# Delta-rule layer of a four-layer decoder trunk: the substitution's transfers move from SyncE's queue to GpSimd's, one per diagonal block, and two of its tiles are used a second time

## The chip, the cores and the metric

The kernel runs on one core of a Trainium2 chip. The metric is device time in microseconds for one execution of the whole program. The time before is 860.16 us, the median of three runs (860.01 to 860.22).

## The reference

Four pre-norm residual layers act on 256 tokens of width 1024, in float32, and a final RMSNorm follows. The layers are a pooling mixer, a gated delta-rule mixer, latent attention, and a pooling mixer again. Only the second layer matters here. For 8 heads, in chunks of 64 tokens, its core is

```python
decay = jnp.exp(jnp.where(causal, diff, -jnp.inf))
L = jnp.where(strict, jnp.einsum('bhnid,bhnjd->bhnij', k_beta, k) * decay, 0.0)
A = jnp.eye(C, dtype=L.dtype) + L
rhs = jnp.concatenate([v_beta, k_beta * jnp.exp(g)[..., None]], axis=-1)
sol = lax.linalg.triangular_solve(A, rhs, left_side=True, lower=True)
```

A scan over the chunks with a 128 x 256 state per head follows. So a unit lower triangular matrix has to be inverted, or a system solved with it, for each head and chunk.

## The kernel before, in words

The 256 tokens are two tiles of 128 (`NT = 2`, index `t`). All weight matrices are streamed from HBM in units of 128 x 512 slices through three raw buffers. ScalarE rounds each slice to a high part (`whi`, line 117), VectorE or, for a few slices, GpSimd makes the low part (`wlo`, line 119), and TensorE does three matmuls per product (lines 127 to 129, and 167). The ring of `whi` and `wlo` has nine slices each. The weight loads are issued by SyncE (SP, line 104).

The delta-rule layer is `gdn_layer`. It works with chunks of 128 tokens, one per tile `t`, so there are 2 x 8 = 16 triangular matrices of 128 x 128. Their transposes lie in `LT` (line 696), written on VectorE at line 692, heads 0 to 3 and then 4 to 7, for both `t`. The inverse is made in two steps.

`substitution` (line 712) inverts the 32 x 32 diagonal blocks, four per matrix, 64 in all. The blocks lie spread over 128 partitions; they are brought together with one block per partition. Eight transfers (line 718, one per `t` and diagonal position `d`) write the blocks of `LT` to the HBM buffer `d_l`, and one transfer (line 721) reads them into `Lb`, 64 partitions x 4 KB. Then GpSimd does forward substitution in 31 rounds of two instructions: a product `pr` (line 726) and a subtraction from `Tb` (line 730). One transfer (line 732) writes `Tb` to the HBM buffer `d_t`, and eight transfers (line 736) bring the inverted blocks back to the diagonals of the two tiles `T[0]` and `T[1]`. All these transfers are issued by SP, in whose queue the weight loads also stand; each queue is issued in order.

`inverses` (line 787) joins the blocks. VectorE transposes `T` to `U` (line 797), and `pairs(t)` (line 803) makes 64 x 64 blocks: TensorE multiplies `LT` by `T` (line 806), VectorE masks the result into `X1` (line 808), TensorE multiplies again (line 812), and VectorE subtracts (line 815). `whole(t)` (line 817) does the same to 128 x 128, at lines 820 to 833. `news` then applies `U[0]` to the values (line 847). `X1` (line 794) is a pair of tiles of their own; a third of each is set to zero by GpSimd (line 796).

The program text lists the steps of the layer in one order:

```python
order = "g0 k0 d a0 g1 k1 a1 s q0 v0 i v1 v2 q1 g2 u0 v3 u1 g3".split()
```

Here `g` are gate projections, `k`, `q`, `v` the projections of keys, queries and values, `a` the making of `LT`, `s` the substitution, `i` the inverses and `u` the use of them. This is only the order in which the instructions are written down. The library's scheduler (`schedule_with_timeline_sim=True`, line 1242) fixes the order of each engine's instructions and of each queue's transfers before the run, by its own prices for every instruction. It also chooses how many buffers a tag gets and where each tile lies (`auto_bufs=True`). On the chip each engine works through its fixed order and waits on semaphores. Tiles made by `big` share the tag `s4` (line 70), whose count is left to the scheduler.

Of the kernel before, what the change touches and what calls it, by code (L numbers as in the profile page):

```python
# [16 lines left out]
P = 128  # L17
D = 1024
S = 256
NT = S // P  # L20
# [22 lines left out]
def trunk(ctx: ExitStack, tc: tile.TileContext, x, positions, norm_g, pool_w_in, pool_w_grp,  # L43
          pool_scale, pool_w_out, gdn_w_in, gdn_conv, gdn_a_log, gdn_dt_bias, gdn_norm_g,
          gdn_w_out, mla_w_in, mla_q_norm_g, mla_w_uq, mla_kv_norm_g, mla_w_ukv, mla_w_out,
          final_g, out, depth=4, final=True):
    nc = tc.nc
# [22 lines left out]
    def big(name, *dims, dt=F32):  # L70
        return s4.tile([P, *dims], dt, tag="s4", name=name)
# [463 lines left out]
    def gdn_layer(i, j, hT):  # L535
        H = GDN_H
        M = NT * H
# [72 lines left out]
        for t in range(NT):  # L610
            nc.gpsimd.dma_start(
                out=Gb[t].rearrange("p h s -> p (h s)"),
# [28 lines left out]
        Q, B = 4, 32  # L641
        Tb = big("Tb", B, B)[:M * Q]
        nc.gpsimd.memset(Tb, 0.0)
        nc.gpsimd.memset(Tb.rearrange("m r c -> m (r c)")[:, ::B + 1], 1.0)
        T = [big("T", H, P) for _ in range(NT)]
        for t in range(NT):
# [48 lines left out]

        LT = [big("LT", H, P) for _ in range(NT)]

# [10 lines left out]
        def lower(hf):  # L708
            for t in range(NT):
                against(LT, kT, s2, hf, t)  # L710

        def substitution():

            d_l = dram.tile([M * Q, B * B], F32, name="d_l")
            lv = d_l.rearrange("(t m d) (r c) -> t d r m c", t=NT, d=Q, r=B)
            for t in range(NT):
                for d in range(Q):
                    nc.sync.dma_start(out=lv[t, d],
                                      in_=LT[t][d * B:(d + 1) * B, :, d * B:(d + 1) * B])
            Lb = big("Lb", B, B)[:M * Q]  # L720
            nc.sync.dma_start(out=Lb, in_=d_l.rearrange("m (r c) -> m r c", r=B))
            pr = small("pr", 256, bufs=1)[:M * Q]
# [8 lines left out]
            d_t = dram.tile([M * Q, B * B], F32, name="d_t")  # L731
            nc.sync.dma_start(out=d_t.rearrange("m (r c) -> m r c", r=B), in_=Tb)
            tv = d_t.rearrange("(t m d) (r c) -> t d r m c", t=NT, d=Q, r=B)
            for t in range(NT):
                for d in range(Q):
                    nc.sync.dma_start(out=T[t][d * B:(d + 1) * B, :, d * B:(d + 1) * B],
                                      in_=tv[t, d])
            nc.vector.reciprocal(rki, rk)
# [48 lines left out]
        def inverses():  # L787
# [5 lines left out]
            U.extend(big("U", H, P) for _ in range(NT))  # L793
            X1 = [big("X1", H, P) for _ in range(NT)]
            for t in range(NT):
# [457 lines left out]
```

## Time and profile before

| | |
|---|---|
| median of three runs | 860.16 us |
| the profiled execution | 859.14 us |
| its span, first to last instruction | 857.4 us |
| mean granted TensorE clock | 0.990 |
| transfers on SP's queue (q1) | 109056 packets, 138.17 MB |
| transfers on GpSimd's queue (q0) | 320 packets, 1.06 MB |
| substitution, first `pr` to last `Tb` | 259.78 to 310.09 us |

The profile is one execution. PE is TensorE's matmuls, PEld its weight loads, DVE is VectorE, ACT ScalarE, POOL GpSimd, SP SyncE; POOLq and SPq are transfer issues on these engines' queues. A group or a timeline row gives the line of the kernel, the operation, what is written from what is read, and the shape; in brackets stand the idle time just before it and what ended it. Tile names in the rows are the program's names with numbers left out, so `X1` is shown as `X`. A row `lhs <- rhs: a, n, b` in the table of waits says that the left waited for the right, a us in total, n times, b us at the longest. A "landing" is the time from a transfer's issue to the arrival of its data. The granted clock is the share of full TensorE speed that the chip allowed.

### The profile page before, as it was taken

Reading aid. Unit: us, or ns where it says so; the run is one execution under the profiler, and the core shown is the slowest. Engines: PE = TensorE matmul, PEld = TensorE weight load, DVE = VectorE, ACT = ScalarE, POOL = GpSimd, SP = SyncE. Lnnn points to the kernel's source line nnn. Section 1 sums busy time; section 2 is a strip of 40 time slices with the busy share of each in tenths; the row PEclk is TensorE's granted clock in tenths of the full one; section 3 lists DMA queues with packets and bytes.
Section 4 is the critical chain, followed back from the end, with each engine's and each line's share of the span. In section 5 each row is a group of like instructions: output and inputs, shape, how many; then the busy total and the mean of one; then the engine's idle time right before and its main releaser. Section 6 shows DMA issues by size and latency. Waiting matters only on the chain.

```text
span 857.4 us, 16137 instructions
## 1 busy us (share of the span) xinstructions
PE 835.0 (97%) x5967; PEld 778.7 (91%) x5967; DVE 591.2 (69%) x1138; ACT 488.2 (57%) x1007; POOL 155.7 (18%) x292
## 2 busy tenths in 40 slices
PE   7999999999999969999999999999999999999996
PEld 6999998988999959888979998999989989999986
DVE  4589776456989665656577659778767668866852
ACT  5565555467857435555565654566555476555542
POOL 4000000233248941022212002000000210000012
PEclk9999999999999989999999999999999999999999
DMA  6765556546555462222547676743652547565551
GB/s 199 249 188 188 178 189 213 180 148 206 188 160 176 134 168 102 75 74 99 173 147 215 201 165 172 196 132 95 171 167 79 173 149 218 175 192 183 187 200 50
DMA packets 111288, 140.43 MB, mean 164 GB/s; under 512 B 23340, under 2 KB 53224, under 8 KB 111208
## 3 DMA queue, kind: packets, MB, share of 16 engines
q1 hardware_dynamic: 109056, 138.17, 53.1%
q8 instruction: 47, 0.77, 0.4%
q0 software_dynamic: 320, 1.06, 0.3%
q10 hardware_dynamic: 1832, 0.16, 0.2%
q14 instruction: 33, 0.27, 0.1%
HBM read 137.79 MB, written 1.58 MB: 163 GB/s over the span
## 4 chain that ended last, share of the span: by engine, by line
PE 85%; POOL 7%; DVE 2%; DMA 2%; issue 2%; ACT 1%; SPq 1%; POOLq 0%; ACTq 0%; DVEq 0%
PE acc L167 34%; PE acc L127 12%; PE acc L128 12%; PE acc L129 12%; POOL Tb L730 2%; POOL pr L726 2%; PE aux L127 2%; PE aux L128 2%; PE aux L129 2%; DVE h L303 1%; DMA gain<-in_norm_g_dram 1%; PE aux L688 1%; ACT junk L209 1%; PE aux L806 1%; PE tp L1165 1%
## 5 line engine op out<-in xcount | busy, mean ns | idle before, releaser
L119 DVE TENSOR_TENSOR wlo<-raw,whi 128x512 fp32r<-128x512 f32 (+1 forms) x491 | 338.6, 712 | 163.2 <-ACT whi L117 160.9
L117 ACT CAST whi<-raw 128x512 fp32r<-128x512 f32 (+1 forms) x508 | 301.4, 617 | 261.8 <-PE acc L167 89.8
L127 PE MATMUL acc<-hTh,whi 128*128 128x256 f32 x832 | 235.3, 283 | 1.0 <-DVE cv L636 1.0
L128 PE MATMUL acc<-hTl,whi 128*128 128x256 f32 x832 | 235.8, 283 | 0.0
L129 PE MATMUL acc<-hTh,wlo 128*128 128x256 f32 x832 | 234.7, 282 | 0.0
L127 PEld LDWEIGHTS acc<-hTh,whi 128*128 128x128 f32 x832 | 157.7, 190 | 1.8 <-issue 1.4
L128 PEld LDWEIGHTS acc<-hTl,whi 128*128 128x128 f32 x832 | 157.6, 189 | 0.4
L129 PEld LDWEIGHTS acc<-hTh,wlo 128*128 128x128 f32 x832 | 157.5, 189 | 0.2
L167 PE MATMUL acc<-wlo,yTh 128*128 128x256 f32 (+1 forms) x384 | 116.2, 319 | 0.0
L167 PE MATMUL acc<-whi,yTh 128*128 128x256 f32 (+1 forms) x384 | 116.2, 323 | 0.0
L167 PE MATMUL acc<-whi,yTl 128*128 128x256 f32 (+1 forms) x384 | 92.4, 321 | 0.0
L167 PEld LDWEIGHTS acc<-wlo,yTh 128*128 128x128 f32 x384 | 72.0, 188 | 5.0
L167 PEld LDWEIGHTS acc<-whi,yTh 128*128 128x128 f32 x384 | 71.9, 188 | 5.2
L167 PEld LDWEIGHTS acc<-whi,yTl 128*128 128x128 f32 x384 | 63.1, 188 | 5.6
L291 POOL TENSOR_TENSOR hg<-x,gain 128x256 f32<-128x256 f32 x18 | 14.8, 832 | 259.1 <-DVE x L353 257.4
L167 PE MATMUL acc<-wlo,hTh 128*128 128x512 f32 (+1 forms) x144 | 55.9, 394 | 0.4 <-DVE wlo L119 0.2
L167 PE MATMUL acc<-whi,hTh 128*128 128x512 f32 (+1 forms) x144 | 55.5, 393 | 0.7 <-ACT hTh L195 0.7
L167 PE MATMUL acc<-whi,hTl 128*128 128x512 f32 (+1 forms) x144 | 45.4, 388 | 0.0
L119 POOL TENSOR_TENSOR wlo<-raw,whi 128x512 fp32r<-128x512 f32 x17 | 23.1, 1360 | 70.2 <-ACT whi L117 70.2
L434 POOL COPY win<-u 128x4 f32<-128x4 f32 x8 | 2.8, 354 | 177.0 <-ACT u L428 177.0
L167 PEld LDWEIGHTS acc<-wlo,hTh 128*128 128x128 f32 x144 | 27.3, 190 | 6.8 <-DVE wlo L119 1.7
L167 PEld LDWEIGHTS acc<-whi,hTh 128*128 128x128 f32 x144 | 27.3, 190 | 6.8 <-ACT hTh L195 1.7
(337 smaller groups left out, 1443.3 us busy)
## 6 DMA issues: line engine op xcount, KB each, us to landing
raw<-in_pool_w_in_dram SPq DMA_DIRECT2D x60, 512.0 KB, 4.4
raw<-in_gdn_w_in_dram SPq DMA_DIRECT2D x48, 512.0 KB, 3.9
raw<-in_pool_w_out_dram SPq DMA_DIRECT2D x32, 512.0 KB, 3.7
raw<-in_mla_w_in_dram SPq DMA_DIRECT2D x24, 512.0 KB, 4.4
raw<-in_mla_w_uq_dram SPq DMA_DIRECT2D x36, 256.0 KB, 3.8
raw<-in_pool_w_grp_dram SPq DMA_DIRECT2D x16, 512.0 KB, 4.2
raw<-in_gdn_w_out_dram SPq DMA_DIRECT2D x16, 512.0 KB, 3.5
raw<-in_mla_w_ukv_dram SPq DMA_DIRECT2D x32, 256.0 KB, 3.4
```

Source lines behind the costliest of these rows:

```text
L117: a = nc.scalar.copy(hi, v)
L119: b = e.tensor_tensor(out=lo, in0=v, in1=hi.bitcast(F32), op=ALU.subtract)
L127: nc.tensor.matmul(o, lhsT=lhs[0], rhs=rhs[0], start=start, stop=False)
L128: nc.tensor.matmul(o, lhsT=lhs[0], rhs=rhs[1], start=False, stop=False)
L129: nc.tensor.matmul(o, lhsT=lhs[1], rhs=rhs[0], start=False, stop=stop)
L167: nc.tensor.matmul(o, lhsT=act(k, t * P, P)[x], rhs=parts[j][z][:, sl], start=k == first and x == z == 0, stop=k == last and x == 1)
L209: nc.scalar.activation(junk[:, :n], src, AF.Square, scale=scale, accum_out=o)
L291: nc.gpsimd.tensor_tensor(out=self.early[t, a], in0=xs[t][:, sl], in1=self.g[:, sl], op=ALU.mult)
L303: nc.vector.scalar_tensor_tensor(out=h[:, cut:], in0=xs[t][:, sl], scalar=r[:, 0:1], in1=self.g[:, sl], op0=ALU.mult, op1=ALU.mult)
L688: nc.tensor.matmul(ps[:, b], lhsT=kT[hf][:, b, tt], rhs=rhs[hf][:, b, tt], start=True, stop=True)
L726: nc.gpsimd.tensor_tensor(out=pv, op=ALU.mult, in0=Lb[:, r, r + 1:, None].to_broadcast([M * Q, n, c]), in1=Tb[:, r:r + 1, :c].to_broadcast ...
L730: nc.gpsimd.tensor_tensor(out=tv, in0=tv, in1=pv, op=ALU.subtract)
```

## The change

The two tiles `T` become halves of one tile `Ts`, and the two tiles `LT` halves of one tile `LTs`. One transfer can then carry the block at diagonal position `d` for both `t` and all heads, so the eight transfers each way become four with twice the bytes. All ten are issued by GpSimd. `Lb` and `Tb` are kept as whole 128-partition tiles, and after the substitution their memory is viewed as `X1`, so that no tiles are made for `X1`.

```diff
-        Tb = big("Tb", B, B)[:M * Q]
+        Tb_ = big("Tb", B, B)
+        Tb = Tb_[:M * Q]
...
-        T = [big("T", H, P) for _ in range(NT)]
+        Ts = big("T", NT, H, P)
+        T = [Ts[:, t] for t in range(NT)]
+
+        def diagonal(a, d):
+
+            return a[d * B:(d + 1) * B, :, :, d * B:(d + 1) * B].rearrange("p t h c -> p (t h) c")
...
-        LT = [big("LT", H, P) for _ in range(NT)]
+        LTs = big("LT", NT, H, P)
+        LT = [LTs[:, t] for t in range(NT)]
...
+        free = []
+
         def substitution():
 
             d_l = dram.tile([M * Q, B * B], F32, name="d_l")
-            lv = d_l.rearrange("(t m d) (r c) -> t d r m c", t=NT, d=Q, r=B)
-            for t in range(NT):
-                for d in range(Q):
-                    nc.sync.dma_start(out=lv[t, d],
-                                      in_=LT[t][d * B:(d + 1) * B, :, d * B:(d + 1) * B])
-            Lb = big("Lb", B, B)[:M * Q]
-            nc.sync.dma_start(out=Lb, in_=d_l.rearrange("m (r c) -> m r c", r=B))
+            lv = d_l.rearrange("(m d) (r c) -> d r m c", d=Q, r=B)
+            for d in range(Q):
+                nc.gpsimd.dma_start(out=lv[d], in_=diagonal(LTs, d))
+            Lb_ = big("Lb", B, B)
+            Lb = Lb_[:M * Q]
+            free.extend((Lb_, Tb_))
+            nc.gpsimd.dma_start(out=Lb, in_=d_l.rearrange("m (r c) -> m r c", r=B))
...
-            nc.sync.dma_start(out=d_t.rearrange("m (r c) -> m r c", r=B), in_=Tb)
-            tv = d_t.rearrange("(t m d) (r c) -> t d r m c", t=NT, d=Q, r=B)
-            for t in range(NT):
-                for d in range(Q):
-                    nc.sync.dma_start(out=T[t][d * B:(d + 1) * B, :, d * B:(d + 1) * B],
-                                      in_=tv[t, d])
+            nc.gpsimd.dma_start(out=d_t.rearrange("m (r c) -> m r c", r=B), in_=Tb)
+            tv = d_t.rearrange("(m d) (r c) -> d r m c", d=Q, r=B)
+            for d in range(Q):
+                nc.gpsimd.dma_start(out=diagonal(Ts, d), in_=tv[d])
...
-            X1 = [big("X1", H, P) for _ in range(NT)]
+
+            X1 = [a.rearrange("p (h a) c -> p h (a c)", h=H) for a in free]
```

## The prediction, made before the result was known

> **What bounds the kernel now.** I read the page's busy table first, then the table by stretches, TensorE's waits, and the timelines of the stretch in which TensorE waits.
>
> ```profile
> PE 835.0 (97%) x5967; PEld 778.7 (91%) x5967; DVE 591.2 (69%) x1138; ACT 488.2 (57%) x1007; POOL 155.7 (18%) x292
> ```
> ```profile
> 190.00:308.70 118.70, 117.73 (x901) 112.24 (x899) 96.38 (x213) 76.17 (x144) 69.88 (x88) 1.00 0.58 176
> 308.70:316.10 7.40, 0.04 (x2) 0.04 (x1) 1.90 (x3) 1.91 (x4) 1.41 (x5) 0.85 0.55 134
> 316.10:324.60 8.50, 8.50 (x42) 8.50 (x43) 4.88 (x6) 3.33 (x9) 0.00 (x0) 0.53 0.66 200
> 324.60:361.00 36.40, 36.40 (x271) 32.11 (x270) 22.91 (x47) 18.77 (x42) 4.86 (x6) 1.00 0.27 88
> 435.00:685.00 250.00, 250.00 (x1786) 232.98 (x1784) 178.64 (x387) 143.35 (x333) 15.97 (x26) 1.00 0.57 161
> 694.00:846.00 152.00, 152.00 (x1141) 145.00 (x1140) 103.92 (x157) 82.95 (x143) 8.50 (x17) 1.00 0.57 181
> ```
> ```profile
> PE aux L806 <- DMA T<-d_t: 7.4, 1, 7.4
> ```
>
> TensorE is the bound. Its column is the first after the width of a stretch; the granted clock is the third from the end. From 435 to 685 and from 694 to 846 us it is never idle, so nothing can be gained there. The one large gap lies in the stretch that the change touches: 7.4 us in which TensorE stands at line 806 and waits for the transfers of T. After it the clock is 0.53 for 8.5 us, which loses 8.5 x 0.47 = 4.0 us. The stall and its aftermath together cost 11.4 us, 1.3% of the time, and this is the most that the change can win.
>
> The chain that ends in the stall:
>
> ```profile
> 248.11 2.14 DVE L692 SCALAR_TENSOR_TENSOR LT<-aux,s,DT 128x128 f32<-128x128 f32 x8
> ```
> ```profile
> 249.25 1.82 SPq L718 DMA_DIRECT2D d_l<-LT  x4
> 251.18 0.39 SPq L104 DMA_DIRECT2D raw<-in_gdn_w_in_dram  x1
> 251.61 1.95 SPq L718 DMA_DIRECT2D d_l<-LT  x4
> ...
> 300.12 5.42 SPq L104 DMA_DIRECT2D raw<-in_gdn_w_in_dram  x3
> 310.12 0.47 SPq L732 DMA_DIRECT2D d_t<-Tb  x1
> 310.68 0.53 SPq L104 DMA_DIRECT2D raw<-in_gdn_w_in_dram  x1
> 313.12 3.78 SPq L736 DMA_DIRECT2D T<-d_t  x8
> ```
> ```profile
> 253.11 2.87 DMA d_l<-LT
> 256.10 3.62 DMA Lb<-d_l
> ...
> 310.12 2.94 DMA d_t<-Tb
> 313.98 2.02 DMA T<-d_t
> ```
> ```profile
> 259.78 0.23 POOL L726 TENSOR_TENSOR pr<-Lb,Tb 64x31 f32<-64x31 f32 x1 [1.25 <-DMA Lb<-d_l]
> ...
> 309.85 0.24 POOL L730 TENSOR_TENSOR Tb<-Tb,pr 64x31 f32<-64x31 f32 x1
> ```
> ```profile
> 308.45 0.28 PE L129 MATMUL acc<-hTh,wlo 128*128 128x256 f32 x1
> 316.09 3.65 PE L806 MATMUL aux<-T,LT 128*128 128x64 f32 x16 [7.36 <-DMA T<-d_t]
> ...
> 326.57 1.89 PE L806 MATMUL aux<-T,LT 128*128 128x64 f32 x16
> ```
>
> LT is whole at 250.25. Eight transfers, one collecting transfer and GpSimd's 62 steps follow, from 259.78 to 310.09, then d_t and eight transfers back, and line 806 starts at 316.09. The second group of 16 matmuls of that line takes 1.89 us where the first took 3.65: that is the clock. TensorE's order is fixed before the run, and it had independent projection matmuls left (they fill 316 to 350). So the stall is not the length of the chain. It is the error of the plan, which put line 806 about 7.4 us too early. A longer chain costs nothing if the plan knows of it; a chain that is longer than planned costs its whole excess.
>
> **The change part by part.** First the real length of the chain. The only transfers that GpSimd issues now give the price:
>
> ```profile
> 206.15 0.80 POOL L608 DMA_DIRECT2D d_g<-grow  x1 [0.95 <-DVE grow L606]
> 208.34 1.09 POOL L611 DMA_DIRECT2D Gb<-d_g  x2 [1.39 <-DMA d_g<-grow]
> ```
> ```profile
> Gb<-d_g POOLq DMA_DIRECT2D x2, 512.0 KB, 6.5
> d_l<-LT SPq DMA_DIRECT2D x8, 32.0 KB, 3.0
> ...
> T<-d_t SPq DMA_DIRECT2D x8, 32.0 KB, 2.0
> ...
> d_g<-grow POOLq DMA_DIRECT2D x1, 8.0 KB, 1.9
> ```
>
> An issue on GpSimd takes 0.80 alone and 1.09/2 = 0.55 behind another; on SP it takes 0.45.
>
> Front: a merged transfer reads both halves of LT, so the first starts at 250.25 and not at 249.25: +1.00. The last of four starts 0.80 + 2 x 0.55 = 1.90 later, at 252.15, and not at 253.11 (eight issues with weight loads among them): -0.96 in all. I keep the landing of 2.87, because nothing shows 64 KB from GpSimd; the bounds are 1.9 (d_g) and 6.5 (Gb, eight times the bytes). Lb pays 0.80 for 0.53 at issue: +0.27, with the same bounds. GpSimd's steps start 0.69 us earlier.
>
> Back: d_t pays 0.80 for 0.47: +0.33. Its data come from GpSimd's own last step, so no other queue is woken. Line 806 needed the first four of eight transfers, 316.09 - 313.12 = 2.97 after the first issue. It now needs all four, since each carries both halves: 1.90 to the last issue and 2.0 to land, 3.90, or +0.93. Altogether the chain is -0.69 + 0.33 + 0.93 = 0.57 us longer. With the landing bounds on the three serial landings it is between about 3 us shorter and 10 us longer; I take 0.57, since SP's own rows show landings of these same blocks.
>
> Second, the plan. The plan is made anew, and its prices are not in the profile. It too must see the wait for both halves and the four transfers back. If it charges each GpSimd issue between the back-to-back 0.55 and the landing 1.9 of d_g, I take 1.0, nearer to the lone issue's 0.80. Then its front grows by 1.00 + 3.0 - 3.86 = 0.14 (3.86 is 253.11 - 249.25), Lb by 0.47, d_t by 0.53, the way back by 3.0 + 2.0 - 2.97 = 2.03, together 3.17. Line 806 then goes 3.17 later in TensorE's order while the chain ends 0.57 later: the stall becomes 7.4 - 2.6 = 4.8 us. The lost clock scaled with it is 4.0 x 4.8/7.4 = 2.6. Gain 2.6 + 1.4 = 4.0 us. At 0.55 for an issue the plan moves by only 0.14 - 1.35 + 0.02 + 0.08 + 2.03 - 1.35 = -0.43 and the stall is 8.4; at 1.9 it moves by over 8 and the stall is gone.
>
> Third, SP is freed. SP stood for 4.8 us in front of d_t, and the weight loads behind it came late:
>
> ```profile
> SPq L732 <- POOL X L796: 4.8, 1, 4.8
> ```
> ```profile
> 309.89 1.14 ACT L117 CAST whi<-raw 128x512 fp32r<-128x512 f32 x2 [1.48 <-DMA raw<-in_gdn_w_in_dram]
> 315.33 1.14 ACT L117 CAST whi<-raw 128x512 fp32r<-128x512 f32 x2 [4.30 <-DMA raw<-in_gdn_w_in_dram]
> ```
>
> ScalarE got no weights between 311.03 and 315.33. This costs nothing by itself now, because TensorE stands at line 806 anyway. But if matmuls are put ahead of line 806, their weights must be there: the change supplies them, and without it the two units cast at 309.89 would last only 24 matmuls of 0.12 us, 2.9 us. So it supports the forecast and adds no term.
>
> Fourth, the second use of Lb and Tb.
>
> ```profile
> 310.04 0.30 POOL L796 MEMSET X<- 128x256 f32 x1
> ```
> ```profile
> 320.13 0.68 DVE L808 TENSOR_TENSOR X<-aux,m 128x512 f32<-128x512 f32 x1
> ```
>
> One memset must now wait until the last step has read Lb, the other until d_t has left Tb (about 313). X1 is first written by line 808 at 320.13, seven microseconds later: nothing. If a memset stands ahead of the four transfers, it costs 0.30. Two tiles of 4 KB a partition come free; where TensorE is never idle, more buffers buy nothing.
>
> New waits: GpSimd now stands before Lb until d_l has landed (some 3 us) and before the T transfers until d_t has landed (3 us). Behind it are its shares of the weight subtractions at line 119, 1.3 us each, and TensorE waits for those. The ring of nine weight slices, 9 x 12 x 0.12 = 13 us of matmuls, covers 3 us.
>
> **The rivals.**
>
> *The stall stays.* The plan moves by no more than the chain does. For it: the front's account is nearly even at every price. Stall 7.4 + 0.57: 860.7 us, between 858.5 and 861.9.
>
> *GpSimd's order holds the first transfers back.* SP could issue d_l while GpSimd stood still; in one queue it cannot.
>
> ```profile
> 252.67 1.70 POOL L119 TENSOR_TENSOR wlo<-raw,whi 128x512 fp32r<-128x512 f32 x1 [4.50 <-ACT whi L117]
> ```
>
> If this subtraction stands ahead of the d_l transfers, they start at 254.37 and not at 250.25: +4.1, and the stall is 7.4 + 0.57 + 4.1 = 12.1. That is 864.8 us, slower. It decides as soon as that one instruction is planned ahead of line 718 and its input comes as late as now. Against it: the plan may see the wait and turn them round.
>
> *Descriptor writing is held up.* The same GpSimd step takes twice as long beside VectorE at some times:
>
> ```profile
> 262.99 0.42 POOL L726 TENSOR_TENSOR pr<-Lb,Tb 64x135 f32<-64x135 f32 x1
> ...
> 303.76 0.83 POOL L726 TENSOR_TENSOR pr<-Lb,Tb 64x135 f32<-64x135 f32 x1
> ```
>
> If issues double like it, the eight that lie on the path (up to each last issue, Lb and d_t) cost 8 x 0.55 = 4.4 more, the plan knows nothing of it, and the time is 860.16 + 0.57 + 4.4 = 865.1 us. The Trainium skill, "SBUF — State Buffer", section "SBUF: two separate sides", speaks for this and against the change: GpSimd writes a transfer's descriptors itself and is locked out while VectorE runs in a two-port mode, so that a transfer of some 620 ns took some 3100 ns beside a VectorE copy. By that figure eight transfers would cost an estimated 8 x 2.5 = 20 us and the time would be about 881 us. Against it stand the rows above: issues of 0.80 and 0.55 us in a stretch in which VectorE was busy throughout (its column is the third after the width).
>
> ```profile
> 205.50:209.50 4.00, 4.00 (x18) 3.19 (x18) 4.00 (x10) 1.66 (x3) 1.94 (x4) 1.00 0.30 72
> ```
>
> *The new plan opens a gap elsewhere.* TensorE is full in 402 of the 411 us from 435 to 846, so any gap there is loss: 2 to 8 us.
>
> **How the numbers follow.** The span is 857.4, the profiled execution 859.14, the median of the runs 860.16; I apply differences to the median. Forecast: 860.16 - 4.0 = 856.2 us, own range 848.8 (stall and slow clock gone) to 858.4. Chances: forecast 0.46, stall stays 0.21, order on GpSimd 0.15, descriptors 0.10, gap elsewhere 0.08. What can be told from no change is 0.2%, 1.7 us. So faster 0.46, same 0.21, slower 0.33. The range of 8 in 10 goes from 850.0 to 866.0: some 0.07 of the forecast's chance lies below it, and the worst of the descriptor and gap cases above it.
>
> **What would show it right or wrong.** Right: TensorE's wait at line 806 at 3 to 6 us, more projection matmuls ahead of it than now, ten issues on GpSimd's queue at 0.55 to 0.8 us, the way from LT whole to the first step of pr at 8 to 10 us. Wrong: a wait at line 806 above 8 us; d_l issued later than 1 us after LT is whole, with a weight subtraction ahead of it; issues above 1.1 us; a TensorE wait for wlo from GpSimd; gaps of TensorE after 361 us that were not there.

## The result, and the profile after

The changed kernel takes 865.09 us (median of four runs, 864.3 to 865.84) and the kernel before, run beside it, 860.09 us (four runs): a ratio of 1.006, 95% interval 1.0043 to 1.0078. The forecast was 856.2 us. The change is 5.0 us slower, within the range of 850 to 866 us, but on the other side of no change. The profiled execution took 864.83 us with a span of 863.1 us, 5.7 us more than the span before, at a mean clock of 0.987.

Line numbers move in the changed kernel: the first transfers are line 727, `Lb` 731, `pr` 736, `Tb` 740, `d_t` 742, `T` 745, the memsets 805, the first pairs matmul 815, and its mask 817. The busy table of the page, and TensorE's waits (line, what ended the wait, us in total, times, longest):

```profile
PE 838.5 (97%) x5967; PEld 780.9 (90%) x5967; DVE 591.0 (68%) x1138; ACT 489.0 (57%) x1007; POOL 159.7 (19%) x302
```
```profile
PE aux L815 <- DMA T<-d_t: 5.8, 1, 5.8
PE acc L127 <- DVE vc L636: 5.1, 1, 5.1
```

The instruction counts of TensorE, VectorE and ScalarE are the same. TensorE still waits for T, 1.6 us less than before, but a second wait of 5.1 us has come. It lies where nothing was edited: in the projection of the values. The table by stretches of the changed kernel, and two of its stretches in the kernel before:

```profile
260.00:276.00 16.00, 10.94 (x81) 10.76 (x80) 16.00 (x40) 8.18 (x17) 13.96 (x26) 0.84 0.44 133
...
312.70:318.50 5.80, 0.06 (x1) 0.00 (x0) 1.99 (x3) 3.22 (x7) 2.03 (x4) 0.71 0.93 264
318.50:327.00 8.50, 8.47 (x46) 8.50 (x47) 3.06 (x3) 1.48 (x5) 0.00 (x0) 0.60 0.09 28
...
435.00:685.00 250.00, 249.56 (x1761) 231.02 (x1760) 178.31 (x386) 144.50 (x337) 15.26 (x24) 1.00 0.56 156
690.00:700.00 10.00, 8.56 (x55) 6.95 (x54) 6.40 (x14) 6.82 (x19) 4.88 (x10) 1.00 0.33 105
```
```profile
260.00:276.00 16.00, 16.00 (x138) 16.00 (x137) 16.00 (x35) 10.82 (x24) 14.51 (x26) 1.00 0.52 153
690.00:700.00 10.00, 9.86 (x47) 7.80 (x48) 6.97 (x12) 8.51 (x17) 0.62 (x2) 1.00 0.48 159
```

TensorE's column is the first after the width, the clock the third from the end, the busy share of the DMA engines the second. From 260 to 276 VectorE is busy without a pause in both kernels; TensorE is full before and stands for 5.06 us after. While it waits for T, the DMA engines are 0.93 busy; in the corresponding wait before it was 0.55. The matmuls at both waits, from TensorE's timeline:

```profile
267.23 0.28 PE L129 MATMUL acc<-hTh,wlo 128*128 128x256 f32 x1
272.58 0.55 PE L127 MATMUL acc<-hTh,whi 128*128 128x256 f32 x1 [5.06 <-DVE vc L636]
...
318.53 3.65 PE L815 MATMUL aux<-T,LT 128*128 128x64 f32 x16 [5.78 <-DMA T<-d_t]
```

The sum of what TensorE loses: before 7.4 at the wait for T and 4.0 by the clock behind it, 11.4 us. After: 5.06 at the new wait; behind it 21 matmuls start every 0.213 instead of 0.119 us, 2.0; 5.8 at the wait for T; and 8.5 x 0.40 = 3.4 by the clock behind that: 16.3 us. That is 4.9 us more. A third, small place is at 690 to 700 us, in the next layer: idle 1.44 instead of 0.14 us, 1.3 more. Together 6.2, for a span that grew by 5.7.

This sum says where TensorE stood, and not what made it stand. After the wait at the bank it came to the pairs and waited for T all the same. Without the 5.06 us and the 2.0 behind them it would, by these rows, have reached the pairs some 7 us sooner and stood there some 7 us longer, unless T too had come sooner. So the loss is better read from the pairs on. From their first matmul to the last of the news (the products with `U[0]`), TensorE is never idle, in the kernel before and in the changed one:

```profile
316.09:360.20 44.11, 44.11 (x306) 39.96 (x307) 27.38 (x53) 21.31 (x48) 4.86 (x6) 0.91 0.35 111
```
```profile
318.53:364.60 46.07, 46.07 (x328) 42.01 (x329) 28.14 (x53) 21.25 (x46) 4.86 (x6) 0.93 0.30 97
```

The stretch begins 2.4 us later, because T is there later. It holds 22 matmuls more, which the plan no longer puts ahead of the pairs, and is 2.0 us longer. These 4.4 us and the 1.3 in the next layer are the 5.7 of the span.

GpSimd's timeline through the substitution:

```profile
250.04 2.70 POOL L727 DMA_DIRECT2D d_l<-LT  x4 [2.39 <-DVE LT L699]
...
256.83 0.56 POOL L731 DMA_DIRECT2D Lb<-d_l  x1 [2.77 <-DMA d_l<-LT]
...
260.55 0.23 POOL L736 TENSOR_TENSOR pr<-Lb,Tb 64x31 f32<-64x31 f32 x1 [1.84 <-DMA Lb<-d_l]
...
307.93 0.24 POOL L740 TENSOR_TENSOR Tb<-Tb,pr 64x31 f32<-64x31 f32 x1
308.47 0.65 POOL L742 DMA_DIRECT2D d_t<-Tb  x1 [0.30 <-POOL Tb L740]
311.80 2.61 POOL L745 DMA_DIRECT2D T<-d_t  x4 [2.68 <-DMA d_t<-Tb]
314.40 0.33 POOL L805 MEMSET Tb<- 128x256 f32 x1
```

And the issues of the way back (form, count, KB each, median us to landing):

```profile
d_t<-Tb POOLq DMA_DIRECT2D x1, 256.0 KB, 3.0
T<-d_t POOLq DMA_DIRECT2D x4, 64.0 KB, 5.8
```

An issue costs 0.56 to 0.68 us and `d_t` lands as it did. T's transfers land in 5.8 us where SP's took 2.0, so the pairs start 6.73 us after the first of them was issued, and not 2.97.

The compiled programs show what the plan did. (Orders and PSUM banks below are read from them, not from the profile.) It put 1505 projection matmuls of lines 127 to 129 ahead of the first pairs matmul, where it had put 1527: 22 fewer. And v2's first accumulator got PSUM bank 0, which holds an accumulator of v0; before, v2 had banks 1 and 2. VectorE's convolution of v0 (the `vc` of the wait) was still reading that bank.

### The profile page after: what moved, and what is told of

It is laid out like the page before. It is cut to its first block, busy times and chain, and to the rows that moved or that the text cites. A ratio compares the mean times of both kernels' runs of the same rounds, so it can differ in the third digit from the quotient of the medians.

```text
span 863.1 us, 16134 instructions
## 1 busy us (share of the span) xinstructions
PE 838.5 (97%) x5967; PEld 780.9 (90%) x5967; DVE 591.0 (68%) x1138; ACT 489.0 (57%) x1007; POOL 159.7 (19%) x302
## 4 chain that ended last, share of the span: by engine, by line
PE 82%; POOL 7%; DVE 4%; DMA 3%; issue 2%; ACT 1%; SPq 0%; POOLq 0%; ACTq 0%; DVEq 0%
PE acc L167 31%; PE acc L127 12%; PE acc L129 12%; PE acc L128 12%; POOL Tb L740 2%; PE aux L127 2%; PE aux L128 2%; PE aux L129 2%; POOL pr L736 2%; DMA raw<-in_pool_w_in_dram 1%; DVE wlo L119 1%; DMA T<-d_t 1%; PE aux L695 1%; PE aux L815 1%; PE tp L1174 1%
## 5 line engine op out<-in xcount | busy, mean ns | idle before, releaser
L167 PEld LDWEIGHTS acc<-whi,hTl 128*128 128x128 f32 x144 | 26.9, 191 | 5.9 <-DVE hTl L200 0.5
```

The costliest lines, as they stand in the source:

```text
L167: nc.tensor.matmul(o, lhsT=act(k, t * P, P)[x], rhs=parts[j][z][:, sl], start=k == first and x == z == 0, stop=k == last and x == 1)
```

## The experiments

The theory after this comparison: the loss has two causes. The new plan gives v2 a bank that VectorE still reads, and T's way back meets weight loads that SP, no longer standing in front of `d_t`, now issues beside it. The rival: GpSimd's queue, merged transfers or the second use of the tiles cost by themselves. A second question is whether the wait for T is time that other matmuls could fill, as the forecast took it. The first half of this theory, that the bank wait costs by itself, did not come out of the runs.

All runs in one table. "Ahead" is the count of projection matmuls ahead of the first pairs matmul, "bank wait" TensorE's wait for `vc`, "T lands" the median landing of T's transfers as far as the profile gives it, "pairs" the start of the first pairs matmul, "end" the start of the last matmul of the news in the profiled execution. From there to the end of the span it is 496 to 499 us in all of them but e9 (501.7), so "end" shows where most of the time was lost.

| run | ratio (95%) | ahead | bank wait | T lands | wait for T | pairs | end |
|---|---|---|---|---|---|---|---|
| before | 1 | 1527 | 0 | 2.0 | 7.4 | 316.1 | 360.2 |
| after | 1.006 (1.0043–1.0078) | 1505 | 5.1 | 5.8 | 5.8 | 318.5 | 364.6 |
| e1 | 0.9995 (0.9986–1.0005) | 1526 | 0 | 1.9 | 6.9 | 318.5 | 361.8 |
| e2 | 1.0003 (0.9987–1.002) | 1530 | 0 | 2.4 | 4.0 | 314.3 | 361.2 |
| e3 | 1.0113 (1.0093–1.0133) | 1584 + gate | 0 | 2.1 | 0 | 332.6 | 372.3 |
| e4 | 1.0035 (1.0024–1.0047) | 1495 | 4.9 | 2.5 | 4.2 | 316.7 | 363.5 |
| e5 | 1.0034 (1.0023–1.0046) | 1569 | 0 | 2.4 | 9.2 | 321.4 | 365.8 |
| e6 | 1.0084 (1.0055–1.0114) | 1584 | 0 | 4.1 | 2.8 | 326.2 | 367.6 |
| e7 | 1.0079 (1.0055–1.0103) | 1584 | 0 | 3.5 | 0 | 326.4 | 367.5 |
| e8 | 1.0077 (1.0062–1.0092) | 1504 | 5.4 | 6.0 | 6.7 | 319.9 | 365.5 |
| e9 | 1.0082 (1.0059–1.0106) | 1565 | 0.4 | 2.4 | 3.2 | 321.0 | 363.0 |
| e10 | 0.9991 (0.9972–1.001) | 1584 | 0 | 2.4 | 3.2 | 322.2 | 364.5 |
| e11 | 1.0059 (1.0043–1.0075) | 1569 | 0 | 4.3 | 4.8 | 326.7 | 365.7 |
| e12 | 1.0059 (1.004–1.0078) | 1553 | 0 | 2.2 | 8.4 | 321.8 | 366.6 |
| e13 | 1.0068 (1.0056–1.0081) | 1548 | 0 | 2.2 | 7.5 | 319.6 | 366.2 |
| e14 | 1.0023 (1.0013–1.0032) | 1534 | 0 | 3.7 | 10.3 | 319.2 | 362.1 |
| e15 | 0.9995 (0.9984–1.0006) | 1568 | 0 | 2.4 | 1.5 | 320.8 | 360.5 |
| e16 | 0.9999 (0.9986–1.0011) | 1544 | 0 | 2.4 | 5.6 | 319.8 | 362.2 |
| e17 | 0.9982 (0.9972–0.9992) | 1543 | 0 | 2.5 | 5.9 | 317.3 | 359.8 |

**One part alone.** e1_reuse_only: the kernel before with the second use of the tiles.

```diff
-            X1 = [big("X1", H, P) for _ in range(NT)]
+            X1 = [a.rearrange("p (h a) c -> p h (a c)", h=H) for a in free]
```

> The kernel before with one part of the change: Lb and Tb become X1; sixteen single transfers on SP as before. Theory A (two things cost the time: a PSUM bank that the new plan gives to the projection v2 while VectorE still reads v0 from it, some 5 us of stall and 2 of slow clock, and T coming back later than the place of the pairs matmul allows): this plan puts 1526 projection matmuls ahead of the pairs matmul where before had 1527, and v2 keeps banks 1 and 2, so 860 us within 1. Rival C (the second use of the tiles is what costs): 864 to 865 us.

859.75 us against 859.98. The second use costs nothing and brings nothing.

e2_merged_on_sp: the changed kernel, with all ten merged transfers on SP.

```diff
-                nc.gpsimd.dma_start(out=lv[d], in_=diagonal(LTs, d))
+                nc.sync.dma_start(out=lv[d], in_=diagonal(LTs, d))
```

> The change with all ten transfers issued by SP again; merged and with the second use. Theory A: no bank clash in this plan (v2 on banks 1 and 2), 1530 projection matmuls ahead, T back within some 3.5 us of its first issue, so one stall of 7 to 8 us at the pairs matmul and 859 to 861 us. Rival C (merging and the second use cost): a second stall and 863 to 866 us. Rival B (the issue by GpSimd itself costs): 860 us too, so this run does not part A from B.

860.31 us. Its way back, and its waits:

```profile
T<-d_t SPq DMA_DIRECT2D x4, 64.0 KB, 2.4
```
```profile
PE aux L815 <- DMA T<-d_t: 4.0, 1, 4.0
PE acc L127 <- DVE cv L636: 3.1, 1, 3.1
```

64 KB in 512 rows of 128 bytes land in 2.4 us from SP, so merging does not explain 5.8. The wait for T is shorter, 4.0 us, and a wait for a convolution (`cv`) ahead of it takes its place. So the loss comes with the change of queue, or with the plan that the change of queue brings.

e3_split_on_pool: the kernel before, its eighteen transfers on GpSimd, not merged.

```diff
-                    nc.sync.dma_start(out=lv[t, d],
+                    nc.gpsimd.dma_start(out=lv[t, d],
```

> The kernel before with its eighteen transfers issued by GpSimd; not merged, X1 of its own. The plan puts 57 projection matmuls and 48 gate matmuls more ahead of the pairs matmul than before, 57 x 0.12 + 48 x 0.234 = 18 us, and v2 gets banks 6 and 7. Theory A: no bank clash, T arrives some 8 us later than before, so no stall at the pairs matmul or under 2 us: 850 to 856 us, unless the inverses then lack work beside them. Rival B (issue by GpSimd costs in itself): more transfers, slower still than the change, 865 to 872 us.

870.4 us, the slowest of all, and again by the plan. It put the whole projection of v3 and the gate's last slice ahead of the pairs. Its waits, GpSimd's timeline and the stretches after:

```profile
PE aux L806 <- ACT vR L781: 3.8, 1, 3.8
PE acc L167 <- POOL wlo L119: 2.9, 1, 2.9
```
```profile
320.75 4.64 POOL L736 DMA_DIRECT2D T<-d_t  x8 [2.88 <-DMA d_t<-Tb]
325.40 1.27 POOL L119 TENSOR_TENSOR wlo<-raw,whi 128x512 fp32r<-128x512 f32 x1
```
```profile
330.00:340.00 10.00, 7.36 (x38) 7.03 (x38) 3.91 (x7) 6.93 (x17) 0.66 (x1) 0.50 0.66 224
340.00:350.00 10.00, 10.00 (x54) 9.38 (x54) 2.71 (x4) 2.57 (x6) 0.61 (x1) 0.50 0.01 2
350.00:360.00 10.00, 8.45 (x50) 7.93 (x51) 7.10 (x15) 3.58 (x8) 2.31 (x4) 0.50 0.00 0
```

A weight subtraction stands behind GpSimd's eight issues and TensorE waits for it, which is the fourth of the "wrong" signs of the forecast. And the inverse runs for over 30 us at a clock of 0.50, with none of the large projection matmuls left beside it. That was the first hint on the second question: what is put ahead of the pairs is missed behind them.

e4_back_on_act: the changed kernel, T's four transfers issued by ScalarE.

```diff
-                nc.gpsimd.dma_start(out=diagonal(Ts, d), in_=tv[d])
+                nc.scalar.dma_start(out=diagonal(Ts, d), in_=tv[d])
```

> The change with only the four transfers back to T issued by ScalarE instead of GpSimd; SP stays free for weight loads. The bank clash stays (v2 on bank 0), 1495 projection matmuls ahead. If the late landing of T (5.4 to 6.1 us each in the change) is GpSimd's way of issuing, they land in 2 to 3 us here and the wait at the pairs matmul, 10 matmuls or 1.2 us earlier in the plan, is 4 to 5 us: 862 to 864 us. If it is the weight loads that SP now issues beside them, they land in 5 to 6 us here too, and the time is that of the change or above, 865 to 867 us.

863.26 us.

```profile
PE acc L127 <- DVE vc L636: 4.9, 1, 4.9
PE aux L815 <- DMA T<-d_t: 4.2, 1, 4.2
```

T lands in 2.5 us and the pairs start at 316.7, as before the change (316.1). The bank wait stays, and so do 3 of the 5 us. But this is not the bank wait alone: the plan also has 32 matmuls fewer ahead than before the change, 3.8 us, and T is 0.6 us later. These two are already more than the 3.3 us by which "end" is late, so the run does not show that the bank wait costs anything.

**Other plans of the changed kernel.** e5_other_shares moves two of v1's weight subtractions on GpSimd to other slices, which makes the plan anew and touches no transfer.

```diff
-                            pool=((1, 3, 5, 7), (3, 7), (), ())[vi])
+                            pool=((1, 3, 5, 7), (1, 5), (), ())[vi])
```

> The changed kernel whole; only two of v1's weight subtractions on GpSimd are those of other slices (1 and 5 in place of 3 and 7). The plan that comes out gives v2's accumulators other banks than v0's (1 and 2, as before the change) and puts 64 more projection matmuls ahead of the first pairs matmul (1569 in place of 1505). Theory A (the loss is the plan's: a bank that VectorE still reads, and an order that asks for T too early): the wait of 5.1 us for VectorE at v2's first matmul is gone with its slow clock (7.2 us together), the 64 matmuls (7.5 us) take its place, so that T is still late by about 5.5 us; about 858 us. Theory B (GpSimd's transfers themselves cost the 5 us, whatever the plan): 864 to 866 us. Theory C (VectorE is simply too late for v2, banks or not): the wait for VectorE near 267 us stays at 4 to 5 us, 864 to 866 us.

863.4 us, a miss for all three: the bank wait is gone, as theory A said, but T came 2.9 us later than in the changed kernel and the wait for it was 9.2 us. It is 1.7 us quicker even so, with 64 more matmuls ahead. Here the weight loads met `d_t` and not T:

```profile
d_t<-Tb POOLq DMA_DIRECT2D x1, 256.0 KB, 5.2
T<-d_t POOLq DMA_DIRECT2D x4, 64.0 KB, 2.4
```

Four kernels can be set side by side: neither cost (before) 0; bank wait with T nearly on time (e4) +3.0 us by the ratio; T late without a bank wait (e5) +2.9; both (after) +5.0. Each edit is a whole new plan, with 1495 to 1569 matmuls ahead, so this is no clean sum and does not part the two.

e6_inverse_last and e7_before_inverse_last put the inverse behind v3 in the list that gives the order, in the changed kernel and in the one before.

```diff
-        order = "g0 k0 d a0 g1 k1 a1 s q0 v0 i v1 v2 q1 g2 u0 v3 u1 g3".split()
+        order = "g0 k0 d a0 g1 k1 a1 s q0 v0 v1 v2 q1 g2 v3 i u0 u1 g3".split()
```

> The changed kernel whole, but the inverse is written behind v3 in the list that gives the order, so all 1584 projection matmuls of lines 127 to 129 stand ahead of the first pairs matmul, 79 more than in the changed kernel, and some 24 of the queries' and transposes; v2's banks are 1 and 2. Theory A (plan): no wait for VectorE at v2, and T, about 318.5 us, is late by no more than 1.5 us; only the 48 matmuls of the gate's last slice stand beside the inverse. 849 to 852 us if they are enough, some 5 us more if gaps open in the inverse as they did when that slice stood ahead of it. Theory B (the transfers by GpSimd cost whatever the plan): above 860 us.

> The kernel before with the same one-line edit of the order: the inverse behind v3, 1584 projection matmuls ahead of the first pairs matmul where it had 1527. 57 x 0.117 = 6.7 us and some 2 us of transposes and attention matmuls take the place of the wait of 7.4 us and its slow clock of 4.0. Theory A: the wait for T is under 1 us and the time 848 to 851 us, within 1.5 us of the changed kernel with this edit. Theory B (GpSimd's transfers cost by themselves): this one gains and the changed kernel with the same edit stays 5 us or more above it.

866.82 and 866.65 us: both slower by the same, a clear miss on the time. The two kernels then differ by nothing, which speaks against the rival, but the gain did not come. In e7 TensorE does not wait for T at all: the last of T's transfers are issued before 317.8, but the pairs start at 326.4, since 24 transposes and attention matmuls came ahead as well, one every 0.11 us, and TensorE waited 2.9 us for `kqT` among them and 1.9 for `gsg`. And from there to the last matmul of the news it takes 41.1 us and not 44.1. About 57 x 0.117 + 24 x 0.11 = 9 us of work were taken out from beside the inverse, and it became 3 us shorter.

**The way back without weight loads.** e8_dt_on_sync issues `d_t` on SP, so that SP stands until GpSimd's last step.

```diff
-            nc.gpsimd.dma_start(out=d_t.rearrange("m (r c) -> m r c", r=B), in_=Tb)
+            nc.sync.dma_start(out=d_t.rearrange("m (r c) -> m r c", r=B), in_=Tb)
```

> The changed kernel whole, but the transfer that writes Tb out is issued on SP's queue; SP then stands there until GpSimd's last step and issues no weight loads meanwhile, so the return of T meets quiet DMA engines. T's own four transfers stay with GpSimd, and the order of TensorE is the same to one matmul (1504 ahead, v2 on v0's bank). If T lands late (5.4 to 6.1 us) because of the weight loads beside it: it lands in 2 to 3 us here, the wait for T is about 2.5 to 3.5 us, and the time about 861 us. If GpSimd's issue of transfers with 512 rows of 128 bytes is slow by itself: it lands in 5 to 6 us, and the time is 864 to 866 us. In both the wait at v2 stays near 5 us.

866.47 us, and T landed in 6.0 us. That looked like the second answer, but the trace shows SP issuing weight loads from 310.20 on, as soon as `d_t` was out; T was issued at 312.77. The return had not been made quiet. In the kernel before, SP stood a second time, from 311.21 to 313.12, in front of T's own transfers until `d_t` had landed; here it does not. e9_quiet_return holds SP until T is there:

```diff
                 nc.gpsimd.dma_start(out=diagonal(Ts, d), in_=tv[d])
+            d_x = dram.tile([P, P], F32, name="d_x")
+            hold.append(nc.sync.dma_start(out=d_x, in_=T[1][:, 7]).ins)
...
+        def gated(vi):
+            with later(*hold):
+                gate(vi)
```

> As the run with Tb's way out on SP, but SP stands still longer: behind that transfer it issues a small one that reads T (64 KB into a scratch tile), and the weight loads of the gate's last slice are held behind it. So no weight load is issued from Tb's way out until T has landed; T's four transfers are GpSimd's, as in the change. If T lands late because of weight loads beside it: it lands in 2.0 to 2.6 us here, where it took 5.8 and 6.0. If GpSimd's issue of these transfers is slow by itself: 5 to 6 us again. The plan puts 1565 projection matmuls ahead of the first pairs matmul, and v2 takes bank 2 first, so the wait at v2 should be gone; with a wait for T of 3 to 4 us the time is 858 to 861 us, with a late landing 862 to 864.

Its landing against that of e8:

```profile
T<-d_t POOLq DMA_DIRECT2D x4, 64.0 KB, 2.4
```
```profile
T<-d_t POOLq DMA_DIRECT2D x4, 64.0 KB, 6.0
```

The same transfers from the same queue land in 2.4 us when no weight load runs and in 6.0 when they do. The time was a miss, 866.23 us: `Lb` landed in 6.5 us in front (3.6 in the changed kernel), and after the news this program lost another 4 us against the others, 1.9 of it in a wait for `h` in the next layer.

e10_after_quiet adds the same to the changed kernel, all ten transfers staying on GpSimd.

> The changed kernel with all transfers of the substitution on GpSimd; only the small SP transfer that reads T is added and the weight loads of the gate's last slice are held behind it. Plan: v2 on banks 1 and 2, all 1584 projection matmuls ahead of the first pairs matmul, but 24 fewer transposes and attention matmuls than in the runs with the inverse written last. Theory (two costs: the clash on v2's bank, and T's return beside the weight loads): neither shows; T lands in 2 to 3 us, the waits for T and for VectorE are under 2 us each. What is left is the thinner cover of the inverse: 857 to 861 us. If GpSimd's queue costs by itself: 864 us or more.

858.46 us, no difference from the kernel before: neither cost shows in the time, though the waits that were to be under 2 us were 3.2 (T) and 2.6 (`cv`) in the profiled execution. The ten executions spread from 856.1 to 863.2 us, and the profiled one lies at the slow end, so its "end" in the table is not that of the median. e15_after_quiet_less_ahead is the same with v1's slices of e5, to tell whether that was the luck of one plan.

> As the changed kernel with the gate's last weight loads held behind T, with the same move in v1: all transfers of the substitution on GpSimd, v2 on banks 1 and 2, 1568 projection matmuls ahead of the first pairs matmul in place of 1584. By the two causes (clash gone, quiet return): T lands in 2.0 to 2.6 us, no wait of over 1.5 us at v2, and the time is 857 to 861 us, 4 us or more under the changed kernel. If the run with 1584 ahead was quick only because of its order: 862 to 866 us.

858.93 us, again level with the kernel before. Its waits and its way back:

```profile
PE acc L127 <- DVE cv L636: 3.5, 1, 3.5
PE aux L817 <- DMA T<-d_t: 1.5, 1, 1.5
```
```profile
T<-d_t POOLq DMA_DIRECT2D x4, 64.0 KB, 2.4
```

So GpSimd's queue need not cost: under another plan and with a quiet return the changed kernel is 6 us quicker than as it was built. T itself came no sooner for it. The pairs start at 320.8, 2.3 us later than in the changed kernel, because `Lb` landed in 6.5 us and the steps took 50.5; what the rows show on the other side is 63 more matmuls ahead of the pairs.

**Is the wait for T to be filled?** e11_before_cover_moved and e12_merged_cover_moved give v0's subtractions 1 and 5 to VectorE, in the kernel before and in e2.

```diff
-                            pool=((1, 3, 5, 7), (3, 7), (), ())[vi])
+                            pool=((3, 7), (3, 7), (), ())[vi])
```

> The kernel before; only v0's weight subtractions 1 and 5 go to VectorE. The plan that comes out has 1569 projection matmuls ahead of the first pairs matmul, 42 more than before (4.9 us), no gate matmul and no other step in front. If the wait for T is lost time that independent matmuls can fill (the forecast's view): the wait falls from 7.4 to about 2.5 us, its slow clock from 4.0 to 1.4, and the time to 853 to 855 us. If what is put ahead is missed beside the inverse (from the first pairs matmul to the last of the news 44 us before, 41 us with only the gate's slice beside it): the wait falls, but at most 3 us come out, 857 to 860 us.

> The merged transfers on SP, with the same move of v0's subtractions 1 and 5 to VectorE: 1553 projection matmuls ahead of the first pairs matmul, where the merged transfers alone had 1530 and waited 4.0 us for T. 23 x 0.117 = 2.7 us fill the wait: T about 1.3 us late, and with the slow clock 4 us less than 860.3: 856 to 858 us. If the cover is missed beside the inverse instead: 859 to 861 us.

864.23 and 863.88 us, misses that did not answer: the added work on VectorE held back the front, and GpSimd's first step came at 267.64 and 263.57 (259.78 before). e11 has a reading of its own. SP issued two weight loads between `d_t` and T, and SP's own transfers were late too (the row has seven of the eight; over all whose landing the profile gives it is 4.3):

```profile
T<-d_t SPq DMA_DIRECT2D x7, 32.0 KB, 4.5
```

e13_before_more_ahead and e14_before_shorter_chain move only a little: v1's slices 1 and 5 in the kernel before, and, in e14, also the two subtractions that stand amid the 62 steps to VectorE.

```diff
-                            pool=((0, 4), (7,), (3, 7), (7,))[vi])
+                            pool=((0, 4), (7,), (), (7,))[vi])
```

> The kernel before; only two of v1's weight subtractions on GpSimd are those of slices 1 and 5 in place of 3 and 7. The plan has 1548 projection matmuls ahead of the first pairs matmul, 21 more (2.5 us), v2 on banks 1 and 2, and nothing that delays LT. If independent matmuls put ahead fill the wait one for one: the wait for T falls from 7.4 to about 4.9 us, the slow clock from 4.0 to 2.6, and the time by 3.9 us to 856 us. If the cover is missed behind, or GpSimd's steps run slower beside a busier VectorE (they took 47.6 us where VectorE was busy for 35.5 us of them and 51.6 where it was busy for 46.3): 859 to 862 us.

> The kernel before with the same move in v1, and the two weight subtractions of the gate's third slice, 1.3 us each and in the midst of the 62 steps, go from GpSimd to VectorE. 1534 projection matmuls ahead, 7 more than before (0.8 us), and the chain 2.6 us shorter by the rows. If the chain through GpSimd sets when T lands: T at about 313.5, the wait for T 7.4 - 2.6 - 0.8 = 4.0 us and the time 855 to 857 us. If VectorE's added work (2.4 us) slows the steps by as much: 859 to 861 us.

865.02 and 860.99 us. In both the first step came some 3 us later than before. In e14 the steps themselves took 48.0 instead of 50.3 us, so the two subtractions were worth 2.3 us there, and the later start took it away. In both, two weight loads stand in SP's queue ahead of the eighth `d_l` transfer: it was issued at 254.10 and 254.42 (253.11 before) and `Lb` at 258.85 and 259.04 (256.10 before). Why the plan puts them there when v1's slices are moved is not known.

e16_front_on_sync_quiet and e17_front_on_sync_plain are e15 and e10 with the first five transfers issued by SP.

> As the last run (weight loads of the gate's last slice held behind T, v1's subtractions 1 and 5), but the way out of LT and the way in of Lb are issued by SP, merged as in the change; only Tb's way out and T's way back stay with GpSimd. If the transfers of the substitution are late only where weight loads run beside them: Lb lands in 3.3 to 3.6 us and not in 6.5, GpSimd's steps begin about 4 us earlier (259.5), and T about 317. The plan has 1544 projection matmuls ahead of the first pairs matmul, 24 fewer (2.8 us), so the gain is between 1 and 4 us: 855 to 858 us, under both kernels. If the front's transfers land late by chance and not by the loads: 858 to 860 us.

> The same with v1's subtractions as in both kernels (3 and 7), so that the changed kernel differs only in the queue of the front's transfers and the held loads: 1543 projection matmuls ahead, v2 on banks 1 and 2. By the same reasons 855 to 859 us; if the choice of v1's slices matters by more than 2 us, this run and the one beside it differ by that.

859.96 us, no difference, and 858.22 us, faster than the kernel before by 0.18% (0.08 to 0.28%). It is the only version that beats both kernels, by about as much as a measurement can tell: the kernel before itself had medians from 859.03 to 860.09 us beside the various runs. Its waits and the landings of the substitution, back and front:

```profile
PE aux L817 <- DMA T<-d_t: 5.9, 1, 5.9
PE acc L127 <- DVE cv L636: 1.3, 1, 1.3
```
```profile
T<-d_t POOLq DMA_DIRECT2D x4, 64.0 KB, 2.5
...
Lb<-d_l SPq DMA_DIRECT2D x1, 256.0 KB, 3.9
```

The steps began at 259.62, as expected. In e16, where two weight loads stand directly ahead of `Lb` on SP and not one, `Lb` took 5.8 us and the steps began at 262.01. The difference of the two is 1.7 us.

**What the table adds up to.** Take from the kernel before its "end" of 360.2, add the delay of "pairs" against 316.1, and take off 0.119 us for every matmul more ahead than 1527. This estimate meets the measured "end" within 1.2 us in nine programs: after, e1, e4, e8, e11, e14, e15, e16 and e17. Among them are all three with a bank wait, which needs no term of its own. In e2, e5, e6, e7, e9, e10, e12 and e13 the end is 2.4 to 5.3 us later than that. (e3 is left out; its plan moved the gate too.) What parts the two groups is the clock from the pairs to the end: 0.91 to 0.94 in the first, 0.75 to 0.88 in the second. In e5, for one, TensorE stands another 1.45 us there, and the clock is 0.80 (0.91 before):

```profile
321.41:365.80 44.39, 42.94 (x265) 38.86 (x266) 21.77 (x42) 16.66 (x38) 5.32 (x6) 0.80 0.19 61
```

What in a plan keeps the clock up behind the pairs is open: e13 with 1548 ahead is in the second group, e15 with 1568 in the first.

## Why the prediction was wrong

1. **The gap is the plan's error, and all of its 11.4 us can be won.** The first half holds: in e15 T came 4.7 us later than before the change, 41 more matmuls stood ahead, the wait was 1.5 us, and the news ended at 360.5 against 360.2. A late T that the plan knows of costs nothing. The second half fails. From the first pairs matmul to the last of the news it took 44.1 us before the change, and however much stood ahead it never took less than 39.0 (e11; 39.7 in e3 with no projection left beside it). With T at 316.1 that leaves an estimated 44.1 - 39.0 = 5.1 us to be won, not 11.4. The forecast looked at the matmuls that fill the wait and not at those that would be missing behind it. No run moved the order with everything else fixed, so the estimate is not shown directly.
2. **The chain, 0.57 us longer.** The issues were right (0.56 to 0.68 us each, `d_t` 3.33 from issue to T's first issue, +0.33 as worked out), but GpSimd stood 0.30 us between its last step and the issue of `d_t`, where SP had followed within 0.03. The front was forecast 0.69 shorter; from LT whole (247.60 + 2.15, the last group of line 699) to the first step it took 260.55 - 249.75 = 10.8 us against 9.53, 1.3 longer: `d_l`, kept at a landing of 2.87, took 4.1, beside weight loads. The way back was forecast at 3.90 and took 6.73: the landing of 2.0 was taken from SP's rows, and was 5.8. The 62 steps, taken as fixed, were 47.6 us and not 50.3. So T was there 2.4 us later. The quicker steps hid nearly half of the 5.6 us that the transfers lost (1.3 in front, 0.6 around `d_t`, 3.8 on the way back); that the total is no worse is luck.
3. **The plan puts the pairs 3.17 us later.** This is the step that turned the sign. It put them 22 matmuls, 2.6 us, earlier, and it remade the PSUM banks far from the edit. A price list for the plan worked out from the profile's durations could say neither. In the forecast's own terms the stall had to become 7.4 + 2.4 + 2.6 = 12.4 us and not 4.8. What TensorE lost ahead of the pairs was 5.06 + 2.0 + 5.8 = 12.9 us: the same stall, of which the bank took the first part. No row of the profile before gave the plan's prices; the 1.0 us for an issue was a choice.
4. **SP freed: no cost.** Wrong. Before the change SP stood in front of `d_t`, and after one more weight load in front of T's transfers, and so kept all but that one load from running while T came back. e8 shows that the first standing alone is not enough (T landed in 6.0 us), and e9 that T lands in 2.4 when no load is issued until it is there. The forecast saw SP's wait of 4.8 us, and read it only as lateness of the weights.
5. **The second use of the tiles: nothing.** Right (e1).
6. **The ring of nine covers GpSimd's waits.** Right here: TensorE waits for no `wlo` of GpSimd's in the changed kernel. In e3, with eight issues, it did (2.9 us), but also in e11 (4.1), with all transfers on SP.

Of the rivals, the one that came nearest had 0.08: a new plan opens a gap elsewhere, 2 to 8 us. It looked for the gap after 435 us, where 1.3 us came, and not at 267. Its condition could not be read from the profile before, but it needed a larger chance wherever a scheduler decides everything anew. Two others named the time almost to the digit, 864.8 and 865.1 us against 865.09, and that is chance, for the condition of neither came. GpSimd's order did not hold `d_l` back: 250.04 is 0.3 us after LT was whole. And descriptor writing was not held up. The Trainium skill, "SBUF — State Buffer", section "SBUF: two separate sides", gave some 3100 ns for a transfer beside a VectorE copy; the issues here took 0.65 us each, also from 250.04 to 252.74, beside VectorE's convolutions and subtractions. A VectorE copy of that kind beside an issue was not seen here. The two steps of 0.42 and 0.83 us that stood for this rival both ran beside a busy VectorE; the difference lay in what it did, as the last section shows.

On the queues, the Trainium skill, "DMA: Bandwidth & Descriptors", section "Issuing engines are not separate DMA queues", states that transfers of all engines interleave on the same DMA engines, and that issuing from several "will only save the time on the sequencer". The runs agree with the first (T in 2.4 us alone, 6.0 beside weight loads). The second is too kind here: the time on SP's sequencer was no waste, because it kept loads back.

What stays open: whether GpSimd's transfers suffer more from the same loads than others. ScalarE's landed in 2.5 us (e4) with loads issued at 310.76 and 315.30, SP's in 4.3 (e11), GpSimd's in 5.8 and 6.0, but the loads differ in each. One load alone does not show: in the kernel before and in e2 one was issued 2.4 us ahead of T and landed in the midst of its way back, and T landed in 2.0 and 2.4 us. That the bank is the cause of the wait of 5.1 us is supported by this: all three programs that gave v2's first accumulator bank 0 waited 4.9 to 5.4 us for `vc`, and no other waited more than 0.4 for it. It was not tried by changing the bank alone. Why the plan put fewer matmuls ahead is open too. The three programs with the bank wait have the fewest (1495 to 1505, all others 1526 or more), so the plan may have reckoned with the wait; no run shows it.

## What to carry to other kernels

When transfers leave a queue, ask what that queue then starts in the meantime: an engine that stands in front of a transfer also keeps its later loads from running beside it. Where a scheduler orders everything, an edit is a new plan; compare the orders and the PSUM banks of the two programs before pricing the edit itself. Of two waits on one engine, one behind the other, the last decides: an earlier one only moves idle time forward, unless it delays what the last one waits for. And a wait in front of a chain of small matmuls is not free room: the large matmuls that would fill it may be what keeps that chain covered and the clock up.

## What the runs showed of the hardware

GpSimd's 62 steps, with six to eight other instructions among them, take 47.6 to 53.1 us, and what VectorE does beside them matters. The steps' own stretches in the changed kernel and in e5 (VectorE is the third column after the width, GpSimd the fifth):

```profile
260.55:308.17 47.62, 42.56 (x306) 40.70 (x305) 35.48 (x70) 24.95 (x49) 43.22 (x69) 0.93 0.42 126
```
```profile
260.68:312.29 51.61, 50.61 (x378) 47.60 (x377) 46.31 (x86) 27.95 (x57) 47.21 (x69) 1.00 0.52 158
```

With VectorE busy for 35.5 us the steps were 4.0 us quicker than with 46.3. It is not the busy share alone. In the kernel before, the same step took 0.42 us at 262.99 and 0.83 at 303.76, and VectorE was busy throughout both. Its own rows at these times:

```profile
262.86 0.86 DVE L636 SCALAR_TENSOR_TENSOR vc<-acc,tap,vc 128x255 f32<-128x255 f32 x2
```
```profile
303.65 3.14 DVE L119 TENSOR_TENSOR wlo<-raw,whi 128x512 fp32r<-128x512 f32 x4
```

Over all the traces this step (64x135) took 0.42 us at the median where VectorE ran convolutions of line 636 or other SCALAR_TENSOR_TENSOR for nine tenths of it or more (22 steps), 0.45 where it ran nothing (12), and 0.84 where it ran the weight subtractions of line 119 as long (11). Those have two inputs in SBUF, while the convolution in the row above reads `acc` from PSUM. So in these traces the steps are slow beside the subtractions, and not beside the convolutions. In the steps' stretch of e5 VectorE spent 27.5 us on TENSOR_TENSOR, in the changed kernel 16.9.

All three runs with the bank wait have steps of 47.6 to 47.8 us; TensorE's standing leaves VectorE with less to do, and so the bank wait seems to have brought T sooner. T's transfers showed a factor of 2.5 between quiet and loaded DMA engines (2.4 and 6.0 us), more than the doubling of their size, which cost 0.4 us (2.0 to 2.4 on SP).
